# Attention block: the sink enters the row maximum as its start value, logits are kept negated, GpSimd makes the low weight parts in quarters, and the gate sigmoids and output splits stand elsewhere

## Chip, cores and metric

The kernel runs on one core of one Trainium2 chip. The metric is device time in microseconds for one launch. The program is one long sequence of engine instructions in a fixed order: TensorE (PE) multiplies, VectorE (DVE), ScalarE (ACT) and GpSimd (POOL) prepare and drain its operands, and SyncE (SP) issues the weight loads.

## What is computed

Two transformer blocks on 512 tokens of width 1024, all in float32. The first block (retention, spatial gating unit, convolutional MLP) is not touched. The second block is where the change lies:

```python
proj = einsum('bld,de->ble', h, w_in[l])
o_a = dsa_branch(a_q, a_k, a_v, i_q, i_k, i_w, topk)   # indexer picks 128 keys per query, causal
o_b = swa_branch(b_q, b_k, b_v, sinks[l])              # window of 128 keys, one sink logit per head
y_a = einsum('ble,ed->bld', o_a, w_branch_a[l])
y_b = einsum('ble,ed->bld', o_b, w_branch_b[l])
mix = sigmoid(g_a) * y_a + sigmoid(g_b) * y_b
x = x + einsum('bld,de->ble', mix, w_out[l])
h2 = rmsnorm(x, mlp_norm_w[l])
u = relu(einsum('bld,df->blf', h2, w_up[l]))
x = x + einsum('blf,fd->bld', u * u, w_down[l])
```

In `swa_branch` the sink is one more logit of every softmax row: it enters the row's maximum and the row's sum, and its own probability is dropped.

## The kernel before

**Split products.** Every large product is made of three TensorE passes over a high and a low part (`mm`, lines 245 to 247). A weight unit (512 KB, 128 partitions x 1024) is loaded into `wr`, ScalarE copies it to the high part `wh` (line 220), and another engine subtracts to get the low part `wl` (line 208, `Stream.flush`). That engine is `W.eng`: VectorE for most of the program, GpSimd from line 1172 to line 1260, that is from the second block's attention up to the end of the product with `w_out_2`. Three raw buffers and five split buffers let the stream run up to three units ahead of TensorE (`LEAD`). Activations are split in the same way by `split` (lines 147 and 148): ScalarE writes the high part, VectorE subtracts for the low part.

**Order.** Nothing is scheduled at run time: the order of instructions on each engine is the order in which the Python program emits them. Class `Weave` holds side tasks (generators) with countdowns; the dense loops call `tick` after a fixed number of matmuls, and a task whose countdown is over emits its next piece there. An attention head pair is such a task (`attend`, line 1052), started every `SWA_EVERY` = 0.75 or `ATT_EVERY` = 0.7 units of dense work; the task waits `LAG_N`, `LAG_T` and `LAG_V` units between its pieces. Each engine runs its own list strictly in order, so an instruction that waits holds all that is behind it on its engine.

**One attend.** For a query tile and two heads: TensorE makes the logits (line 1019); VectorE adds the mask, writes the logits to `pr` and takes the row maximum `mx` (line 1072, one instruction for each head); in the window branch it takes the maximum with the sink (line 1075); it negates the maximum to `nm` (line 1077); ScalarE makes exp(logit + nm) with row sums (line 1080); in the window branch VectorE makes sink + nm and ScalarE its exponential `es` (lines 1084, 1085), which VectorE adds to `sums` (line 1088); VectorE takes the reciprocal `rs` (line 1090); ScalarE scales the rows (line 1092); TensorE transposes (line 1101), ScalarE copies the result to `pT` (line 1103), TensorE multiplies with the values (line 1110), and `put` drains that product: in the window branch by `split` into `ob`, in the other branch by a copy into `oaT` (line 1215), which is split in four pieces after all attends are done (line 1227).

**Around the attends.** The dense work that covers them: the remaining projections, the gate logits `Y` (line 1211), the product with `w_branch_b_2` (line 1217) and the gate logits `Ya` (line 1223). `gate` copies each feature tile of logits out of PSUM (line 1205) and after every fourth applies the sigmoid to 128x2048 values at once (line 1207); exp and sigmoid need different tables on ScalarE, so a sigmoid between exponentials brings two table loads. After the attends come the product with `w_branch_a_2` (line 1243), whose `ev` multiplies by the gate (VectorE, line 1233), adds `Y` (GpSimd, line 1234) and splits the sum into `mh` and `ml`; then the product with `w_out_2` (`down`, line 1259), whose first unit needs the features in order and whose last tiles start the norms `norm_T` for `w_up_2` (lines 466 to 489).

## Time and profile before

| | us |
|---|---|
| median of 3 runs | 1611.67 (1609.97 to 1612.4) |
| profiled execution, time | 1611.67 |
| profiled execution, span from first to last instruction | 1609.9 |
| TensorE busy | 1579.2 (98%) |
| VectorE busy | 765.8 (48%) |
| ScalarE busy | 614.1 (38%) |
| GpSimd busy | 329.8 (20%) |

The profiled execution's time equals the median; 1.8 us of it lie around the span. TensorE's share of busy time is modelled from pipelined matmuls, so a stall shows best as idle time with the instruction that ended it, and as a granted clock below 1.00 in a stretch. The granted clock has two levels, 2.4 GHz (1.00) and 1.2 GHz (half); a mean of 0.96 over a stretch mixes the two.

### The profile page before, as it was taken

What the parts mean: (1) busy time and instruction counts of PE and PEld (TensorE: products, weight loads), DVE (VectorE), ACT (ScalarE), POOL (GpSimd) and SP (SyncE); (2) the same over time, 40 slices, a digit from 0 to 9 for tenths busy, and PEclk for the clock granted to TensorE, in tenths of its full rate; (3) what the DMA queues carried; (4) which work ended last, traced back from release to release, by engine and by line L of the source; (5) the groups of instructions that cost most, each with busy time, mean ns of one, the idle gap of its engine ahead of it and who ended that gap; (6) DMA issues with size and microseconds to landing.
All of it is one profiled execution on the core that took longest, in us unless ns stands there. A gap on an engine that the chain in (4) does not pass through costs nothing.

```text
span 1609.9 us, 19821 instructions
## 1 busy us (share of the span) xinstructions
PE 1579.2 (98%) x7868; PEld 1323.8 (82%) x7868; DVE 765.8 (48%) x1315; ACT 614.1 (38%) x1014; POOL 329.8 (20%) x292
## 2 busy tenths in 40 slices
PE   9999999999999999999999999999999999999998
PEld 8888888888888888888888887777877988888886
DVE  4247322453546544456336788768543322233333
ACT  4233223322324433344234366675833322333222
POOL 1015000341003221212004443333245210110000
PEclk9999999999999999999999999999999999999999
DMA  6322333212442233334321412222233333333221
GB/s 184 118 92 66 92 118 91 69 54 89 131 144 59 86 96 101 92 92 140 126 92 49 143 53 53 79 58 75 66 119 103 92 105 88 96 121 97 97 92 53
DMA packets 187249, 151.77 MB, mean 94 GB/s; under 512 B 5218, under 2 KB 157410, under 8 KB 186644
## 3 DMA queue, kind: packets, MB, share of 16 engines
q1 hardware_dynamic: 185648, 145.06, 29.8%
q0 software_dynamic: 1504, 5.44, 1.0%
q8 instruction: 62, 1.02, 0.3%
q14 instruction: 31, 0.25, 0.0%
q10 hardware_dynamic: 4, 0.00, 0.0%
HBM read 146.29 MB, written 4.19 MB: 93 GB/s over the span
## 4 chain that ended last, share of the span: by engine, by line
PE 82%; DVE 8%; ACT 4%; issue 2%; POOL 2%; ACTq 0%; POOLq 0%; DVEq 0%
PE ps L245 25%; PE ps L247 25%; PE ps L246 25%; PE ps L279 1%; ACT pr L1080 1%; DVE work L1036 1%; PE ps L1019 1%; PE ps L1110 1%; ACT wh L220 1%; PE ps L487 1%; POOL Ya L1234 1%; PE ps L772 1%; DVE sums L1088 1%; PE ps L1101 1%; POOL rstd L460 1%
## 5 line engine op out<-in xcount | busy, mean ns | idle before, releaser
L220 ACT ACTIVATE wh<-wr 128x1024 fp32r<-128x1024 f32 (+1 forms) x259 | 270.8, 1051 | 249.5 <-PE ps L247 131.1
L208 DVE TENSOR_TENSOR wl<-wr,wh 128x1024 fp32r<-128x1024 f32 (+1 forms) x212 | 258.0, 1227 | 174.5 <-ACT wh L220 174.4
L245 PE MATMUL ps<-wh,ls 128*128 128x512 f32 x432 | 168.2, 389 | 0.0
L247 PE MATMUL ps<-wh,ls 128*128 128x512 f32 x432 | 168.1, 389 | 0.0
L246 PE MATMUL ps<-wl,ls 128*128 128x512 f32 x432 | 168.1, 389 | 0.0
L208 POOL TENSOR_TENSOR wl<-wr,wh 128x1024 fp32r<-128x1024 f32 x47 | 114.5, 2445 | 134.5 <-ACT wh L220 127.7
L245 PE MATMUL ps<-h2Th,wh 128*128 128x512 f32 (+1 forms) x352 | 132.7, 377 | 0.0
L246 PE MATMUL ps<-h2Tl,wh 128*128 128x512 f32 (+1 forms) x352 | 132.7, 377 | 0.0
L247 PE MATMUL ps<-h2Th,wl 128*128 128x512 f32 (+1 forms) x352 | 132.7, 377 | 0.0
L245 PE MATMUL ps<-hTh,wh 128*128 128x512 f32 (+1 forms) x256 | 97.7, 382 | 0.0
L247 PE MATMUL ps<-hTh,wl 128*128 128x512 f32 (+1 forms) x256 | 96.4, 376 | 0.0
L246 PE MATMUL ps<-hTl,wh 128*128 128x512 f32 (+1 forms) x256 | 96.2, 376 | 0.0
L245 PE MATMUL ps<-h3Th,wh 128*128 128x512 f32 (+1 forms) x256 | 96.2, 376 | 0.0
L246 PE MATMUL ps<-h3Tl,wh 128*128 128x512 f32 (+1 forms) x256 | 96.2, 376 | 0.0
L247 PE MATMUL ps<-h3Th,wl 128*128 128x512 f32 (+1 forms) x256 | 96.2, 376 | 0.0
L247 PEld LDWEIGHTS ps<-wh,ls 128*128 128x128 f32 x432 | 81.1, 188 | 16.8
L246 PEld LDWEIGHTS ps<-wl,ls 128*128 128x128 f32 x432 | 81.1, 188 | 16.8
L245 PEld LDWEIGHTS ps<-wh,ls 128*128 128x128 f32 x432 | 81.1, 188 | 16.7
L903 ACT ACTIVATE hid<-ps,cols 128x512 f32<-128x512 f32 x44 | 34.3, 780 | 142.2 <-PE ps L247 142.2
L904 DVE SCALAR_TENSOR_TENSOR hid<-ps,cols,hid 128x511 f32<-128x511 f32 x44 | 33.0, 750 | 114.3 <-ACT hid L903 114.3
L911 POOL TENSOR_TENSOR act<-hid 128x512 f32<-128x512 f32 x22 | 46.1, 2094 | 192.3 <-DVE hid L906 176.7
L246 PEld LDWEIGHTS ps<-h2Tl,wh 128*128 128x128 f32 x352 | 66.3, 188 | 12.2
(316 smaller groups left out, 3297.9 us busy)
## 6 DMA issues: line engine op xcount, KB each, us to landing
wr<-in_w_in_dram SPq DMA_DIRECT2D x86, 512.0 KB, 3.8
wr<-in_w_up_dram SPq DMA_DIRECT2D x76, 512.0 KB, 4.0
wr<-in_w_down_dram SPq DMA_DIRECT2D x54, 512.0 KB, 3.6
wr<-in_w_out_dram SPq DMA_DIRECT2D x16, 512.0 KB, 3.7
wr<-in_w_sgu_o_dram SPq DMA_DIRECT2D x8, 512.0 KB, 4.2
wr<-in_w_ret_o_dram SPq DMA_DIRECT2D x8, 512.0 KB, 4.2
g<-in_rows_dram POOLq DMA_DIRECT2D x6, 512.0 KB, 7.3
x<-in_x_dram SPq DMA_DIRECT2D x4, 512.0 KB, 5.7
```

The lines of the kernel that those rows point to most:

```text
L208: eng.tensor_tensor(lo, self.raw.pop(i), hi.bitcast(F32), ALU.subtract)
L220: nc.scalar.activation(hi, self.raw[self.n_hi], AF.Copy)
L245: nc.tensor.matmul(q, lhs[0], rhs[0], start=start, stop=False)
L246: nc.tensor.matmul(q, lhs[0], rhs[1], start=False, stop=False)
L247: nc.tensor.matmul(q, lhs[1], rhs[0], start=False, stop=stop)
L279: nc.tensor.matmul(q[:, :256], wslice(u, k, 0, P)[i], act.at(k, 0, 256)[j], start=(i + j + k == 0), stop=(i == 1 and k == K - 1))
L460: nc.gpsimd.tensor_tensor(r, r, nhalf, ALU.pow)
L487: nc.tensor.transpose(q[:, i * P:(i + 1) * P], xn[:, k * P:(k + 1) * P], ident)
L772: nc.tensor.matmul(o, kz[:, d, c - d, :], vc[c], start=True, stop=True)
L903: nc.scalar.activation(o, q, AF.Identity, bias=col("conv_b", f), scale=col("conv_w1", f))
L904: nc.vector.scalar_tensor_tensor(o[:, 1:], q[:, :T - 1], col("conv_w0", f), o[:, 1:], ALU.mult, ALU.add)
L911: nc.gpsimd.tensor_tensor(act[fa // 4][:, fa % 4, :], a, b, ALU.mult)
```

## The change

- **Sink and sign.** The instruction that adds the mask now multiplies by -1 and takes the minimum, so `pr` holds negated logits and its row result is already `nm`. In the window branch its start value is the negated sink (`nsink`, made once, 128x8), so the sink is in the extremum from the start. Lines 1075 and 1077 go away. The exponential runs with scale -1. The sink's exponential is made by ScalarE from `sinkb` with bias `nm`, one 128x1 instruction for each head, so line 1084 goes away and line 1085 becomes two instructions.
- **Quarters.** While `W.eng` is GpSimd, each low weight part is made by four instructions on 128x256 instead of one on 128x1024.
- **`W.eng`** goes back to VectorE ahead of the product with `w_branch_a_2`, no longer behind the product with `w_out_2`.
- **Gate sigmoids of `Ya`** are no longer applied inside the dense loop: the first half's stands after all attends, the second half's behind feature 1 of the product with `w_branch_a_2`. Those of `Y` stay.
- **Output splits.** Each attend of the first branch writes its result at once as high and low part (`oa`), so `oaT` and the four splits behind the attends go away.
- **Last tile.** For the last query tile of that branch VectorE scales the rows, no longer ScalarE.
- **`ATT_EVERY`** goes from 0.7 to 0.65.

```diff
-ATT_EVERY = 0.7
+ATT_EVERY = 0.65
...
-                eng = nc.gpsimd if i in ON_POOL else self.eng
-                eng.tensor_tensor(lo, self.raw.pop(i), hi.bitcast(F32), ALU.subtract)
+                raw = self.raw.pop(i)
+                if self.eng is nc.gpsimd and i not in ON_POOL:
+
+                    w = hi.shape[1] * hi.shape[2] // 4
+                    l_, r_, h_ = (a.rearrange("p k n -> p (k n)") for a in (lo, raw, hi.bitcast(F32)))
+                    for p_ in range(4):
+                        s = slice(p_ * w, (p_ + 1) * w)
+                        nc.gpsimd.tensor_tensor(l_[:, s], r_[:, s], h_[:, s], ALU.subtract)
+                else:
+                    eng = nc.gpsimd if i in ON_POOL else self.eng
+                    eng.tensor_tensor(lo, raw, hi.bitcast(F32), ALU.subtract)
...
+    nsink = const.tile([P, 8], F32, name="nsink")
+    nc.vector.tensor_scalar(nsink, sinkb, -1.0, None, op0=ALU.mult)
...
-        mx = sm(2, "mx")
+        nm = sm(2, "nm")
         for i in range(2):
             q = ps()
             scores(q, qT, 2 * j + i, t, (kT[0][:, g], kT[1][:, g]), k0 * P, n)
             nc.vector.tensor_tensor_reduce(
-                pr[i][:, :n], q[:, :n], mask, 1.0, -3.0e38, ALU.add, ALU.max, mx[:, i:i + 1])
-        if br == 1:
-            nc.vector.tensor_tensor(mx, mx, sinkb[:, 2 * j:2 * j + 2], ALU.max)
-        nm = sm(2, "nm")
-        nc.vector.tensor_scalar(nm, mx, -1.0, None, op0=ALU.mult)
+                pr[i][:, :n], q[:, :n], mask, -1.0,
+                nsink[:, 2 * j + i:2 * j + i + 1] if br == 1 else 3.0e38, ALU.add, ALU.min, nm[:, i:i + 1])
         sums = sm(2, "sums")
         for i in range(2):
-            nc.scalar.activation(pr[i][:, :n], pr[i][:, :n], AF.Exp, bias=nm[:, i:i + 1],
+            nc.scalar.activation(pr[i][:, :n], pr[i][:, :n], AF.Exp, bias=nm[:, i:i + 1], scale=-1.0,
                                  accum_out=sums[:, i:i + 1])
         if br == 1:
             es = sm(2, "es")
-            nc.vector.tensor_tensor(es, sinkb[:, 2 * j:2 * j + 2], nm, ALU.add)
-            nc.scalar.activation(es, es, AF.Exp)
+            for i in range(2):
+                nc.scalar.activation(es[:, i:i + 1], sinkb[:, 2 * j + i:2 * j + i + 1], AF.Exp,
+                                     bias=nm[:, i:i + 1])
...
         for i in range(2):
-            nc.scalar.activation(pr[i][:, :n], pr[i][:, :n], AF.Copy, scale=rs[:, i:i + 1])
+            if br == 0 and t == NT - 1:
+                nc.vector.tensor_scalar(pr[i][:, :n], pr[i][:, :n], rs[:, i:i + 1], None, op0=ALU.mult)
+            else:
+                nc.scalar.activation(pr[i][:, :n], pr[i][:, :n], AF.Copy, scale=rs[:, i:i + 1])
...
-    def gate(dst):
+    def gate(dst, now=True):
...
-            if f % 4 == 3:
+            if now and f % 4 == 3:
                 nc.scalar.activation(dst[f // 4], dst[f // 4], AF.Sigmoid)
...
-    oaT = bigt([P, 4, T], "oaT")
+    oa = Branch()
     att = wv.spawn(stagger(
-        [attend(0, t, j, lambda j, a, b, q: nc.vector.tensor_copy(oaT[:, j, a:b], q))
+        [attend(0, t, j, lambda j, a, b, q: split(oa.hi[:, j, a:b], oa.lo[:, j, a:b], q))
...
-    dense_a(a_units(w_in_2, 2120, 8), hT2, gate(Ya))
+    dense_a(a_units(w_in_2, 2120, 8), hT2, gate(Ya, False))
     wv.finish([att, idx_task])
-    oa = Branch()
-    for j in range(4):
-        split(oa.hi[:, j, :], oa.lo[:, j, :], oaT[:, j, :])
+    nc.scalar.activation(Ya[0], Ya[0], AF.Sigmoid)
+    W.eng = nc.vector
...
         split(h_[:, f % 4, :], l_[:, f % 4, :], ya(f))
+        if f == 1:
+            nc.scalar.activation(Ya[1], Ya[1], AF.Sigmoid)
...
     down(w_out_2, KD, mix_pair, fin)
-    W.eng = nc.vector
```

The order moves in three places. The line numbers in the second fence of each are those of the changed kernel.

ScalarE at the end of the attends, from the last row scalings or weight copies to the first high part of the mix (`mh`), before and now:

```order
L1092 ACTIVATE pr<-pr,rs 128x512 x2
L1103 ACTIVATE pT<-ps 128x512 x2
L1205 ACTIVATE Ya<-ps 128x512
L1207 ACT_TABLE_LOAD
L1207 ACTIVATE Ya<-Ya 128x2048
L1103 ACTIVATE pT<-ps 128x512 x2
L147 ACTIVATE obh<-oaT 128x512 x4
L147 ACTIVATE mh<-Ya 128x512
```

```order
L147 ACTIVATE obh<-ps 128x128
L1116 ACTIVATE pT<-ps 128x512 x2
L1218 ACTIVATE Ya<-ps 128x512
L1116 ACTIVATE pT<-ps 128x512 x2
L147 ACTIVATE obh<-ps 128x128 x2
L1238 ACT_TABLE_LOAD
L1238 ACTIVATE Ya<-Ya 128x2048
L147 ACTIVATE mh<-Ya 128x512
L229 ACTIVATE wh<-wr 128x1024
L147 ACTIVATE mh<-Ya 128x512
L1250 ACTIVATE Ya<-Ya 128x2048
```

The table load and the sigmoid stood ahead of the last two copies to `pT`; now they stand behind the last attend's output copies, and the second sigmoid behind the second `mh`.

The low weight parts inside the product with `w_branch_a_2`: GpSimd before, VectorE now (GpSimd keeps only the eight additions there):

```order
L208 TENSOR_TENSOR wl<-wr,wh 128x1024 x20
L386 DMA g<-in_rows_dram 128x1024 x2
L1234 TENSOR_TENSOR Ya<-Ya,Y 128x512 x2
L208 TENSOR_TENSOR wl<-wr,wh 128x1024
L1234 TENSOR_TENSOR Ya<-Ya,Y 128x512 x2
```

```order
L148 TENSOR_TENSOR obl<-ps,obh 128x128 x3
L1245 TENSOR_TENSOR Ya<-Ya,ps 128x512
L148 TENSOR_TENSOR ml<-Ya,mh 128x512
L1245 TENSOR_TENSOR Ya<-Ya,ps 128x512
L148 TENSOR_TENSOR ml<-Ya,mh 128x512
L217 TENSOR_TENSOR wl<-wr,wh 128x1024
L1245 TENSOR_TENSOR Ya<-Ya,ps 128x512
```

Each `wl` leaves GpSimd's row of additions and stands on VectorE behind every second `ml`, ahead of the next feature's multiplication with the gate.

VectorE in the norms of the last two token tiles ahead of `w_up_2`, before and now:

```order
L1255 TENSOR_TENSOR xs<-xs,ps 128x512
L478 SCALAR_TENSOR_TENSOR xn<-xs,rstd,g 128x1024
L1255 TENSOR_TENSOR xs<-xs,ps 128x512
L148 TENSOR_TENSOR h3Tl<-ps,h3Th 128x4x128 x2
L1255 TENSOR_TENSOR xs<-xs,ps 128x512
L478 SCALAR_TENSOR_TENSOR xn<-xs,rstd,g 128x1024
L208 TENSOR_TENSOR wl<-wr,wh 128x1024
L148 TENSOR_TENSOR h3Tl<-ps,h3Th 128x4x128 x2
```

```order
L1269 TENSOR_TENSOR xs<-xs,ps 128x512
L487 SCALAR_TENSOR_TENSOR xn<-xs,rstd,g 128x1024
L1269 TENSOR_TENSOR xs<-xs,ps 128x512
L217 TENSOR_TENSOR wl<-wr,wh 128x1024 x2
L148 TENSOR_TENSOR h3Tl<-ps,h3Th 128x4x128 x2
L1269 TENSOR_TENSOR xs<-xs,ps 128x512
L487 SCALAR_TENSOR_TENSOR xn<-xs,rstd,g 128x1024
L217 TENSOR_TENSOR wl<-wr,wh 128x1024
L148 TENSOR_TENSOR h3Tl<-ps,h3Th 128x4x128 x2
```

Two low weight parts, which GpSimd made before, now stand ahead of the third tile's `h3Tl` and so ahead of the fourth tile's `xn`.

## Rows read from the trace of the kernel before

**Rows 1.** The page, part 1: busy us (share of the span) xinstructions of each engine.
```profile
PE 1579.2 (98%) x7868; PEld 1323.8 (82%) x7868; DVE 765.8 (48%) x1315; ACT 614.1 (38%) x1014; POOL 329.8 (20%) x292
```

**Rows 2.** Stretch, length; busy us (x) of PE, PEld, DVE, ACT, POOL; granted clock; DMA.
```profile
960.00:1080.00 120.00, 111.22 (x671) 90.10 (x670) 90.37 (x296) 76.04 (x195) 41.54 (x22) 1.00 0.22 62
...
1080.00:1160.00 80.00, 80.00 (x452) 64.38 (x452) 55.71 (x157) 53.88 (x123) 26.10 (x11) 1.00 0.24 67
...
1160.00:1240.00 80.00, 75.04 (x373) 60.31 (x372) 26.78 (x39) 32.94 (x49) 38.80 (x24) 0.96 0.36 119
```

**Rows 3.** Who waited for whom, PE: us in total, times, longest us.
```profile
PE ps L1101 <- ACT pr L1092: 3.8, 3, 3.1
```

**Rows 4.** Timeline, 987 to 1012 us: start us, us, engine, what [idle before <-releaser].
```profile
987.55 0.17 DVE L1077 TENSOR_SCALAR nm<-mx 128x2 f32<-128x2 f32 x1
...
1001.92 0.74 POOL L510 TENSOR_TENSOR rk<-rope 128x256 f32<-128x256 f32 x1 [5.10 <-DVE rope L504]
...
1004.56 4.70 POOL L208 TENSOR_TENSOR wl<-wr,wh 128x1024 fp32r<-128x1024 f32 x2
...
1005.73 1.24 DVE L1075 TENSOR_TENSOR mx<-mx,sinkb 128x2 f32<-128x2 f32 x1
1007.00 2.29 DVE L1077 TENSOR_SCALAR nm<-mx 128x2 f32<-128x2 f32 x1
...
1009.38 0.51 ACT L1080 ACTIVATE pr<-pr,nm 128x256 f32<-128x256 f32 x1 [4.28 <-DVE nm L1077]
...
1011.46 0.41 PE L493 MATMUL ps<-ident,rk 128*128 128x128 f32 x2 [2.86 <-ACT pT L1103]
```

**Rows 5.** Groups by line, VectorE and ScalarE, 930 to 1215 us: busy us, mean ns.
```profile
L1077 DVE TENSOR_SCALAR nm<-mx 128x2 f32<-128x2 f32 x32 | 19.1, 596 | 1.1
...
L1088 DVE TENSOR_TENSOR sums<-sums,es 128x2 f32<-128x2 f32 x16 | 11.3, 704 | 0.0
...
L1049 DVE TENSOR_SCALAR work<-work 128x512 f32<-128x512 f32 x1 | 0.4, 419 | 0.0
...
L1085 ACT ACTIVATE es<-es 128x2 f32<-128x2 f32 x16 | 3.0, 188 | 0.0
```

**Rows 6.** Timeline, end of the attention, 1171 to 1177 us: ScalarE, then TensorE.
```profile
1171.06 1.28 ACT L1207 ACT_TABLE_LOAD   x1
1172.35 1.91 ACT L1207 ACTIVATE Ya<-Ya 128x2048 f32<-128x2048 f32 x1
1174.16 1.07 ACT L1103 ACTIVATE pT<-ps 128x512 f32<-128x512 f32 x2
...
1174.80 1.15 PE L1110 MATMUL ps<-pT,va 128*64 128x128 f32 x16 [2.35 <-ACT pT L1103]
...
1176.93 0.61 PE L246 MATMUL ps<-obl,wh 128*128 128x512 f32 x1 [0.56 <-DVE obl L148]
```

**Rows 7.** Timeline, product with w_branch_a_2 and after, 1181 to 1214 us.
```profile
1181.35 0.69 DVE L1233 TENSOR_TENSOR Ya<-Ya,ps 128x512 f32<-128x512 f32 x1 [2.66 <-PE ps L247]
...
1184.72 0.68 DVE L1233 TENSOR_TENSOR Ya<-Ya,ps 128x512 f32<-128x512 f32 x1
1187.46 2.21 DVE L148 TENSOR_TENSOR ml<-Ya,mh 128x512 fp32r<-128x512 f32 x1 [2.06 <-ACT mh L147]
1189.59 0.68 DVE L1233 TENSOR_TENSOR Ya<-Ya,ps 128x512 f32<-128x512 f32 x1
...
1211.42 9.85 POOL L208 TENSOR_TENSOR wl<-wr,wh 128x1024 fp32r<-128x1024 f32 x4
...
1213.84 0.50 PE L246 MATMUL ps<-wl,mh 128*128 128x512 f32 x1 [1.80 <-POOL wl L208]
```

**Rows 8.** Timeline, last norms ahead of w_up_2, 1251 to 1258 us.
```profile
1251.96 1.29 DVE L148 TENSOR_TENSOR h3Tl<-ps,h3Th 128x512 fp32r<-128x512 f32 x2 [0.85 <-ACT h3Th L147]
...
1257.29 1.22 DVE L208 TENSOR_TENSOR wl<-wr,wh 128x1024 fp32r<-128x1024 f32 x1
...
1257.52 1.06 PE L487 MATMUL ps<-ident,xn 128*128 128x128 f32 x8
```

## The prediction

> **What bounds the kernel now.** I read the page first: TensorE is busy for 1579.2 us, 98% of the span, and no other engine passes half [rows 1]. So the change can only win what TensorE loses by waiting, or by running at the lower clock level. The table by stretch then shows where that is in the second block [rows 2]: from 960 to 1080 us (window attention) TensorE is busy for 111.22 of 120 us, so 8.8 us are idle; from 1080 to 1160 us (the other attention branch, under dense work) it is never idle; from 1160 to 1240 us it is idle for 5.0 us and the granted clock is 0.96. A mean of 0.96 over 80 us is 0.04 x 80 = 3.2 us of lost array time, at the 1.2 GHz level. Together 17 us lie open in places the change touches.
>
> Third, the timeline says why. Around 1005 us VectorE's `mx`, two numbers per partition, takes 1.24 us, and `nm`, just as small, takes 2.29 us, though it took 0.17 us at 987.55 us [rows 4]. Over the stage `nm` has a mean of 596 ns and `sums` one of 704 ns [rows 5]. In the same microseconds GpSimd makes two low weight parts, 4.70 us in all [rows 4]: `mx` ends as the first of them ends (1004.56 + 2.35 = 1006.9 us), `nm` as the second ends (1009.26 us). So some VectorE instructions stand still until GpSimd's current instruction is over. ScalarE's exponential then starts at 1009.38 us after 4.28 us of idle time, and TensorE waits 2.86 us for a PSUM buffer that ScalarE has not drained [rows 4]. The largest other wait of this kind is for ScalarE's row scaling, 3.8 us in three waits, the longest 3.1 us, at the first window attend [rows 3].
>
> **The sum, part by part.** The profiled execution took 1611.67 us, which is also the median of the runs; the sum starts there.
>
> *Window attention.* Sixteen `mx`, 32 `nm` and 16 sink additions leave VectorE, and what still stands still does so behind a quarter. A quarter costs 0.74 us by the 128x256 addition [rows 4], so the longest single wait falls from 2.4 to about 0.7 us. At 1011.46 us the chain was `mx`, then `nm`, then the exponential: both are gone, so I count all 2.9 us. Of the 3.1 us at the first attend I count 1.1: three small instructions at about 0.2 us, and half a microsecond less of standing still for the indexer's accumulation ahead of them. Of the other 2.8 us (8.8 less these two) I count a third, 0.9 us, since the sigmoids of `Y`, with their table loads, stay in the ScalarE queue there. That makes 4.9 us. I give back 0.9: TensorE arrives sooner at the next late operand, and ScalarE gains sixteen instructions of 188 ns for the second sink exponential, 3.0 us over the stage [rows 5]. **-4.0 us.** Bounds: -7.9 (all but 0.9 of the idle time), and +2 if the quarters bring more waits than the three instructions removed.
>
> *End of the attends.* Before, ScalarE loads the sigmoid table (1.28) and makes the sigmoid (1.91) ahead of the last two copies to `pT`; TensorE waits 2.35 us for them, then 0.56 us for the first split of `oaT` [rows 6], and runs at the lower level afterwards, half of the 3.2 us above: 1.6 us. That is 4.5 us. Now these copies stand ahead of the table load, and three quarters of the output are split before the last attend ends. What stays is the way from the last transposes through two copies (1.07 us for both [rows 6]), about half covered by the product of the attend before: 0.5 us. **-4.0 us.** Bounds: -4.5 and -1 (the clock falls all the same, and 2 us of waits stay).
>
> *Product with `w_branch_a_2`.* The chain is serial: VectorE multiplies, GpSimd adds, ScalarE rounds, VectorE subtracts. A feature takes 3.37 us (1181.35 to 1184.72), a pair 8.24 us (to 1189.59), because one `ml` stands still for GpSimd's weight part and takes 2.21 us, where a VectorE instruction of that shape takes 0.69 [rows 7]. The weight part of the third unit of `w_out_2` is the first of the four that start at 1211.42 us; it ends near 1213.9 us, 32.5 us after the chain began, and TensorE waits 1.80 us for it [rows 7] and pays the other 1.6 us at the lower level. Now VectorE makes the weight part (1.22 us [rows 8]) inside the same chain: a pair is 2 x 3.37 + 1.22 = 7.96 us, and that third unit is ready after 3 x 7.96 + 2 x 3.37 + 1.22 = 31.8 us, only 0.7 us sooner. Against that the chain starts later: 1.28 + 1.91 us of table load and sigmoid now stand behind the last output copy, 3.7 us with the 0.5 us of copies before them, where the first feature's product is there after about 2.8 us (an estimate: 12 passes of 512 columns at 2.4 GHz, and 0.2 us on the way); that is 0.9 us later. **+0.2 us**: the stall of 1.8 us and its lower clock stay. Bounds: -3.4 (both go) and +1.6.
>
> The Trainium skill, "ScalarE: Activation LUTs", section "What ACT_TABLE_LOAD costs", adds to the 1283 ns of the load a drain of about 1380 ns at every switch; by it the sigmoid would end 1.4 us later, and the sum would be 1.4 us worse. The trace disagrees: the sigmoid starts 0.01 us after the load ends [rows 6].
>
> *Norms ahead of `w_up_2`.* Two weight parts of 1.22 us move onto VectorE between the third tile's `xn` and its `h3Tl`. `h3Tl` had 0.85 us of idle time ahead of it, so 2.4 - 0.9 = 1.5 us of delay go down to the fourth tile's `xn`, which ended just ahead of the weight part at 1257.29 us and which TensorE's transposes took up at 1257.52 us, with no slack [rows 8]. **+1.4 us.** Bounds: 0 and +2.4.
>
> *The rest at nothing.* The second branch's attends now use ScalarE and VectorE for each output split; from 1080 to 1160 us these are busy for 53.88 and 55.71 of 80 us [rows 2], and two table loads and a sigmoid leave ScalarE there. The last tile's row scaling on VectorE costs 419 ns a piece by the 128x512 `L1049` [rows 5], in a stretch where that engine has run out of key searches. If this cover were gone, each such step would be paid as in the window stage. `nsink` is one instruction of about 0.2 us. `ATT_EVERY` shifts early attends only; the last four wait for the key search.
>
> Sum: -4.0 - 4.0 + 0.2 + 1.4 = -6.4, so **1605.3 us**, 0.4% faster. Its own range is 1602.5 to 1608. A measurement of this kernel can tell about 0.2%, 3.2 us, from no change.
>
> **The rivals.**
>
> *A, the stalls go more fully.* Window stage -7.2, end of the attends -4.5, and the 1.8 us stall with its clock loss (-3.4) goes because the chain starts on time; norms +1.4. Sum -13.7: 1598.0 us. For it: the idle times are there [rows 2]. Against: the chain's arithmetic gives only 0.7 us.
>
> *B, quarters do not let VectorE in between.* Then what is left (`sums`, splits, accumulations) stands still for 4 x 0.74 = 3.0 us instead of 2.4, and the window stage gains only 1.0 us from the instructions removed. Sum -1.0 - 4.0 + 0.2 + 1.4 = -3.4: 1608.3 us. Against it: `mx` ran at the boundary between two back-to-back GpSimd instructions [rows 4]. The Trainium skill, "GPSIMD Engine Reference", section "2.1 Instruction dispatch", says that a GpSimd core begins the next instruction as soon as its own share is done, without waiting for the other cores, so that boundary need not be free; by that rule rival B would be the case, and the trace agrees only in that GpSimd lost almost nothing there (2 x 2.35 us).
>
> *C, the change does not do what it says.* TensorE meets the next late operand everywhere, and the sigmoid behind the attends stalls the mix as much as it stalled the attends: window -1, end -1, mix +0.2, norms +1.4. Sum -0.4: 1611.3 us.
>
> *D, slower: GpSimd falls behind.* Its 32 weight parts of the stage cost 2.96 instead of about 2.4 us each, more if every quarter first lets a VectorE instruction finish. If a unit's low part then lands 0.5 us too late for TensorE, 32 x 0.5 = 16 us are added to 1605.3: 1621; at 0.3 us, 1614.9 us, which I take. It decides once a part takes longer than TensorE spends on a unit, about 245 / 32 = 7.7 us. Against: GpSimd is busy for 41.54 of 120 us there [rows 2], and units are prepared three ahead.
>
> **How the numbers follow.** Chances: forecast 0.54, A 0.15, B 0.13, C 0.09, D 0.09. Range 1598.0 to 1610.5: from A's time up to between B and C; it leaves out C, D and the lower half of A's spread, with parts of their weight inside. Faster by over 0.2%: the forecast, A, and somewhat over half of B, 0.77. Within 0.2%: C and the rest of B, 0.14. Slower: D, 0.09.
>
> **What would show it.** Right: 128x256 weight parts near 0.74 us on GpSimd; `sums` well below 704 ns; idle time of TensorE from the first attend to 1080 us at 4 to 5 us; no wait above 1 us for `pT` at the last attend, and no low clock there; a wait of about 2 us for `wl` in the product with `w_out_2`; about 1.4 us in front of the fourth tile's transposes. Wrong: waits for `wl` from GpSimd inside the attention (D); VectorE instructions of 2 us beside quarters (B); idle time of TensorE between 1080 and 1160 us.

## The result, and the profile after

The changed kernel takes 1594.7 us (median of 4 runs, 1592.59 to 1595.24) against 1612.01 us before (4 runs, 1609.97 to 1612.4): a ratio of 0.9899 with an interval of 0.9887 to 0.9912. It is 17.3 us faster where 6.4 were forecast, and below the forecast range of 1598.0 to 1610.5. The profiled execution took 1595.02 us, with a span of 1593.3 us.

First the page of the changed kernel, part 1, which answers to [rows 1]:

```profile
PE 1573.6 (99%) x7868; PEld 1321.3 (83%) x7868; DVE 740.3 (46%) x1268; ACT 613.6 (39%) x1032; POOL 317.3 (20%) x376
```

TensorE's busy time fell by only 5.6 us, the span by 16.6: the rest was idle time. VectorE's fell by 25.5 us, although it now makes 224 low weight parts and not 212, each of some 1.2 us. It has 47 instructions fewer, and many that are left must have become shorter.

Second the stretches of the changed kernel, with the columns of [rows 2]. The work now comes some 10 us earlier, so 960 to 1070 answers to 960 to 1080 before.

```profile
960.00:1070.00 110.00, 108.98 (x668) 89.53 (x667) 69.37 (x247) 81.17 (x210) 49.26 (x64) 1.00 0.25 68
1070.00:1150.00 80.00, 80.00 (x455) 64.27 (x454) 47.73 (x150) 51.16 (x133) 29.46 (x42) 1.00 0.24 67
1150.00:1170.00 20.00, 20.00 (x144) 16.30 (x142) 5.29 (x14) 11.78 (x21) 7.21 (x10) 1.00 0.58 211
1195.00:1200.00 5.00, 3.00 (x14) 2.12 (x13) 3.42 (x4) 2.52 (x3) 0.88 (x1) 1.00 0.12 6
```

In the window attention 8.8 us of idle time have become 1.0. Up to 1170 us TensorE never stops again. At 1195 us it stops for 2.00 us, and the clock stays at 1.00; at 1240 us it stops for 1.32 us (the line is shown with the norms, below).

Third, who waited for whom, the waits of TensorE in the changed kernel, which answer to [rows 3]:

```profile
PE ps L496 <- DVE xn L487: 5.8, 7, 1.4
...
PE ps L255 <- DVE wl L217: 3.5, 2, 2.0
...
PE ps L1114 <- ACT pr L1105: 1.0, 1, 1.0
```

The 3.8 us for `pr` are 1.0, one wait at the first window attend. The 2.00 us at 1195 are a wait for `wl`, now VectorE's.

The time can be placed by the start of the same matmuls in both timelines, because TensorE's work between them is the same. "Scores" is the first window score product, "PV" the last window product with the values, "branch a" the first matmul with `w_branch_a_2`, "w_out" its first matmul with `mh`. The norms' stage runs from the last of these to the last matmul of `w_up_2`. The first two landmarks, the kernel before and then the changed kernel:

```profile
957.81 0.56 PE L1019 MATMUL ps<-bkT,bqT 128*128 128x128 f32 x4
...
1070.05 0.66 PE L1110 MATMUL ps<-pT,work 128*64 128x128 f32 x8
```

```profile
957.12 0.56 PE L1030 MATMUL ps<-bkT,bqT 128*128 128x128 f32 x4
...
1059.97 0.66 PE L1123 MATMUL ps<-pT,work 128*64 128x128 f32 x8
```

| us between | before | after | change | forecast |
|---|---|---|---|---|
| scores to PV | 112.24 | 102.85 | -9.4 | -4.0 |
| PV to branch a | 105.82 | 103.23 | -2.6 | |
| branch a to w_out | 24.35 | 21.91 | -2.4 | -4.0, with the row above |
| w_out, first to last `mh` | 49.80 | 47.89 | -1.9 | +0.2 |
| last `mh` to last `h3T` | 177.80 | 179.07 | +1.3 | +1.4 |

That makes -15.0 of the span's -16.6. Another 0.8 come between the second block's first transposes of `xn` (878.73 us before, 878.84 after) and the scores. There the kernel before has this wait of TensorE. Two small VectorE instructions (`ik`, 128x64) had taken 2.03 and 2.32 us beside two weight parts of GpSimd, 0.38 and 0.65 us in the changed kernel, and `hl` came behind them:

```profile
920.43 0.63 PE L493 MATMUL ps<-ident,hl 128*128 128x128 f32 x4 [0.79 <-DVE hl L148]
```

The wait is there (0.67 to 0.82 us) in every kernel below in which GpSimd makes the parts whole or in halves, and in none with quarters. The remaining 0.8 lie in what follows `w_up_2` and in code that the change does not touch, and are less than runs of one kernel differ by (2.4 us before).

### The profile page after: what moved, and what is told of

The parts are those of the page before. It is cut to its first block, busy times and chain, and to the rows that moved or that the text cites. A ratio compares the mean times of both kernels' runs of the same rounds, so it can differ in the third digit from the quotient of the medians.

```text
span 1593.3 us, 19894 instructions
## 1 busy us (share of the span) xinstructions
PE 1573.6 (99%) x7868; PEld 1321.3 (83%) x7868; DVE 740.3 (46%) x1268; ACT 613.6 (39%) x1032; POOL 317.3 (20%) x376
## 4 chain that ended last, share of the span: by engine, by line
PE 90%; DVE 4%; ACT 2%; POOL 2%; issue 2%; ACTq 0%; POOLq 0%; DVEq 0%
PE ps L254 27%; PE ps L256 27%; PE ps L255 27%; PE ps L1030 1%; PE ps L1123 1%; PE ps L1114 1%; PE ps L502 1%; PE ps L288 1%; POOL Ya L1246 1%; PE ps L781 1%; ACT junk L475 1%; POOL rstd L469 1%; DVE wl L217 1%; PE ps L496 1%; DVE y L533 1%
## 5 line engine op out<-in xcount | busy, mean ns | idle before, releaser
L217 DVE TENSOR_TENSOR wl<-wr,wh 128x1024 fp32r<-128x1024 f32 (+1 forms) x224 | 272.4, 1227 | 177.0 <-ACT wh L229 176.9
L214 POOL TENSOR_TENSOR wl<-wr,wh 128x256 fp32r<-128x256 f32 x128 | 94.9, 774 | 112.0 <-ACT wh L229 102.9
L256 PEld LDWEIGHTS ps<-h2Th,wl 128*128 128x128 f32 x352 | 66.2, 188 | 12.3
```

What stands on the lines that cost most here:

```text
L214: nc.gpsimd.tensor_tensor(l_[:, s], r_[:, s], h_[:, s], ALU.subtract)
L217: eng.tensor_tensor(lo, raw, hi.bitcast(F32), ALU.subtract)
L256: nc.tensor.matmul(q, lhs[1], rhs[0], start=False, stop=stop)
```

## The experiments

Each run stands against the kernel before on the same chip: 1610.83 us for the four that have one or more parts of the change alone, 1609.79 for the halves, the end moves without `W.eng`, `W.eng` alone and the spacing, 1609.47 for the rest. Theory 1 is the prediction's: a VectorE instruction of some kinds stands still until GpSimd's current instruction is over. Theory 2 is that the attends gained because their chain has fewer instructions.

### The parts of the change alone

**Quarters alone**, on the kernel before:

```diff
-                eng.tensor_tensor(lo, self.raw.pop(i), hi.bitcast(F32), ALU.subtract)
...
+                    for p_ in range(4):
+                        s = slice(p_ * w, (p_ + 1) * w)
+                        nc.gpsimd.tensor_tensor(l_[:, s], r_[:, s], h_[:, s], ALU.subtract)
```

> The kernel before with GpSimd's low weight parts in quarters and nothing else. Theory 1 (some VectorE instructions stand still until GpSimd's current instruction is over, and that is what TensorE waited for in the window attention): the longest standing time falls from 2.4 to 0.75 us, nm's mean from 596 to under 300 ns, and about 6 us of the window stage's 10 us go: 1606 us. Theory 2 (the gain comes from three fewer instructions in each attend's chain, and the standing is hidden by queues): 1612 us, within 1.5 us of before, or slower by the 0.5 us more that each part costs GpSimd.

Measured: 1600.88 us, 9.95 below before, ratio 0.994 (0.9928 to 0.9953). The groups of this kernel, 930 to 1180 us, with the columns of [rows 5]:

```profile
L1086 DVE TENSOR_SCALAR nm<-mx 128x2 f32<-128x2 f32 x32 | 8.1, 252 | 1.1
...
L1097 DVE TENSOR_TENSOR sums<-sums,es 128x2 f32<-128x2 f32 x16 | 5.2, 327 | 0.0
...
L214 POOL TENSOR_TENSOR wl<-wr,wh 128x256 fp32r<-128x256 f32 x115 | 84.6, 768 | 114.3 <-ACT wh L229 105.5 <-PE ps L1119 8.7
```

Not one instruction left VectorE, and yet scores to PV takes 105.56 us, 6.7 less, although the clock was at 0.67 from 965 to 970 us, behind a wait at the first attend. (What the stage would take at the full clock is not shown: the kernel with `W.eng` alone, below, lost twice that clock there and took no longer for it.) `nm` fell from 596 to 252 ns and `sums` from 704 to 327 [rows 5]. Theory 2 cannot give this; Theory 1's 6 us for the stage are near, and what the time won beyond them lies elsewhere (see the halves). The price is GpSimd's: a quarter takes 768 ns, so four take 3.07 us where one piece took 2.43 (the 29 pieces there before were busy for 70.2 us, the 115 quarters for 84.6), and no wait for a `wl` of GpSimd came up in the attention.

**Sink and sign alone**, on the kernel before:

```diff
-            nc.vector.tensor_tensor(mx, mx, sinkb[:, 2 * j:2 * j + 2], ALU.max)
...
-        nc.vector.tensor_scalar(nm, mx, -1.0, None, op0=ALU.mult)
...
+                pr[i][:, :n], q[:, :n], mask, -1.0,
+                nsink[:, 2 * j + i:2 * j + i + 1] if br == 1 else 3.0e38, ALU.add, ALU.min, nm[:, i:i + 1])
```

> The kernel before with the sink as start value and negated logits, and nothing else. Theory 1: the 16.7 us that nm and mx stood still leave VectorE, so about 6 us are gained here too, and the two parts overlap: 1606 us. Theory 2: this part alone makes the whole window gain, 10 us: 1602 us. If neither holds (the instructions were not on the path): 1611 us.

Measured: 1603.15 us, 7.7 below before, ratio 0.9956 (0.9943 to 0.9968). Scores to PV takes 105.13 us, 7.1 less, although `sums` still takes 712 ns. The time lies between Theory 1's 1606 and Theory 2's 1602 and decides nothing by itself; with the quarters' run, where no instruction went, the account is that the two parts remove the same loss in two ways: one shortens the stand of `mx` and `nm`, the other takes these two out of the chain. So each brings about 7 us alone in that stage, and the whole change 9.4.

**The whole change without quarters:**

```diff
-                if self.eng is nc.gpsimd and i not in ON_POOL:
...
-                else:
-                    eng = nc.gpsimd if i in ON_POOL else self.eng
-                    eng.tensor_tensor(lo, raw, hi.bitcast(F32), ALU.subtract)
+                eng = nc.gpsimd if i in ON_POOL else self.eng
+                eng.tensor_tensor(lo, self.raw.pop(i), hi.bitcast(F32), ALU.subtract)
```

> The changed kernel with whole low weight parts on GpSimd, 128x1024 each. Theory 1: sums and the splits with two SBUF inputs stand still for up to 2.4 us again, sums' mean returns to about 700 ns, and 3 to 4 us are lost: 1598 us. Theory 2: 1595 us, as the changed kernel.

Measured: 1597.56 us, ratio 0.9917 (0.9903 to 0.993), 13.3 below before. On top of the rest, the quarters are worth 2.3 us from scores to PV (105.15 against 102.85), and nothing in the four stages behind it, which agree within 0.02 us.

**The end moves alone** (sigmoids, output splits, last tile's scaling, `W.eng`, `ATT_EVERY`), on the kernel before:

```diff
-ATT_EVERY = 0.7
+ATT_EVERY = 0.65
...
-    dense_a(a_units(w_in_2, 2120, 8), hT2, gate(Ya))
+    dense_a(a_units(w_in_2, 2120, 8), hT2, gate(Ya, False))
...
+    nc.scalar.activation(Ya[0], Ya[0], AF.Sigmoid)
+    W.eng = nc.vector
```

> The kernel before with the last part of the change alone: gate sigmoids of Ya and output splits moved, W.eng back to VectorE earlier, rows of the last tile scaled on VectorE, ATT_EVERY 0.65; whole weight parts and the old sink and sign. Both theories: the window stage stays as it was, and the end gains what the landmarks of the two traces show behind the window stage, 17.3 - 10.1 = 7 us: 1605 us. Should the low clock at the end of the attends come back, 1607 us.

Measured: 1607.47 us, ratio 0.9982 (0.9973 to 0.9991), 3.4 below before. That is the time of the second expectation but not its cause, for the clock stays up at the end of the attends. From branch a on it is the changed kernel (21.90, 47.86 and 179.07 us). From PV to branch a it takes 105.95 us, no less than before: there TensorE waits 0.94 us for a `pT` at 1137.6 us, where whole weight parts meet the closer spacing of the attends. With the old spacing and the same whole parts (end moves without `W.eng` and `ATT_EVERY`, below) this stretch takes 103.73 us. In the run above, which has the closer spacing and adds sink and sign, that wait is gone.

### How long is a stand, and who stands

**Halves**, on the kernel before: the edit of the quarters with 2 in place of 4, shown here against the kernel with quarters alone.

```diff
-                    w = hi.shape[1] * hi.shape[2] // 4
+                    w = hi.shape[1] * hi.shape[2] // 2
...
-                    for p_ in range(4):
+                    for p_ in range(2):
```

> The kernel before with GpSimd's low weight parts in two halves, nothing else. Theory 1 (a VectorE instruction stands still until GpSimd's current instruction ends): the mean of nm falls in proportion between 596 ns (one piece) and 252 ns (four), to 350 to 420 ns, and sums from 704 to 430 to 520 ns. For the time there are two readings of it: 1a, the loss of TensorE grows with the length of the longest stand: half of the 10 us that the quarters won, 5 us below before. 1b, the attends have some slack, and a stand costs only beyond it: then halves win nearly all, 8 to 10 us below before.

Measured: 1599.94 us, ratio 0.9935 (0.9923 to 0.9946), 9.85 below before. The groups of this kernel, 930 to 1180 us:

```profile
L1086 DVE TENSOR_SCALAR nm<-mx 128x2 f32<-128x2 f32 x32 | 12.3, 384 | 1.1
...
L1097 DVE TENSOR_TENSOR sums<-sums,es 128x2 f32<-128x2 f32 x16 | 7.1, 446 | 0.0
...
L214 POOL TENSOR_TENSOR wl<-wr,wh 128x512 fp32r<-128x512 f32 x58 | 76.2, 1336 | 122.1 <-ACT wh L229 122.1
```

With pieces of 2.43, 1.34 and 0.77 us `nm` takes 596, 384 and 252 ns, and `sums` 704, 446 and 327: the stand follows the length of GpSimd's piece. The time does not: halves win 6.1 us from scores to PV and quarters 6.7 (106.16 and 105.56 us, with a like stretch at the lower clock in both). TensorE's wait of 2.86 us at 1011 us [rows 4] is gone with halves as with quarters, and the one at the first attend, 3.06 us before, is 2.11 us with quarters and, in the kernel with halves,

```profile
966.36 0.62 PE L1110 MATMUL ps<-ident,pr 128*128 128x128 f32 x2 [2.40 <-ACT pr L1101]
```

That fits reading 1b: an attend has slack, and only a stand beyond it costs. The totals of the two runs say less, because they hold more than this stage: in these profiles 2.3 us of the quarters' gain and 3.6 of the halves' lie ahead of the second block, in code that neither edit touches, and another 2.6 and 3.7 between first and last `mh`.

**Everything on VectorE**, on the changed kernel:

```diff
-    W.eng = nc.gpsimd
```

> The changed kernel, but all low weight parts are made by VectorE in one instruction each, in the attention too. Theory 1 (the window stage lost its time to VectorE standing still behind GpSimd): sums near 0.17 us, no long stands; but 14 parts of 1.22 us enter VectorE's queue from 960 to 1070 us (69 + 17 = 86 of 110 us busy), each a delay of up to 1.2 us for what is behind it, less than the 2.4 us of GpSimd's whole part and more than its quarter: 1595 to 1598. Theory 2 (the gain came from the shorter chain of small instructions, and VectorE's load is what counts): VectorE is the busiest engine there again, and the window stage gives back most of its 10 us: 1601 to 1606.

Measured: 1597.07 us, ratio 0.9922 (0.9908 to 0.9937), 12.4 below before. First the stretches, then the groups from 930 to 1180 us of this kernel:

```profile
960.00:1070.00 110.00, 109.78 (x671) 90.09 (x670) 80.67 (x259) 80.53 (x209) 8.90 (x8) 1.00 0.25 68
1070.00:1150.00 80.00, 77.82 (x437) 61.44 (x436) 57.00 (x152) 48.73 (x128) 0.00 (x0) 1.00 0.25 67
```

```profile
L217 DVE TENSOR_TENSOR wl<-wr,wh 128x1024 fp32r<-128x1024 f32 x30 | 36.5, 1217 | 0.7 <-ACT wh L229 0.5
...
L1098 DVE TENSOR_TENSOR sums<-sums,es 128x2 f32<-128x2 f32 x16 | 3.4, 215 | 0.0
```

From 960 to 1070 us VectorE is busier than in the changed kernel (80.67 against 69.37 us), and scores to PV is the shortest of all, 102.16 us, with no wait of TensorE: neither GpSimd's help nor a low load was needed there, only that nothing stands for long. The loss came behind it: PV to branch a takes 106.54 us, 3.3 more than in the changed kernel. In that stage TensorE waits three times for `pT`, 1.7 us in all, while VectorE's busy time has gone up from 47.73 to 57.00 of 80 us.

### The end of the attends, and the lower clock

**The end moves without `W.eng` and `ATT_EVERY`**, on the kernel before:

```diff
-    dense_a(a_units(w_in_2, 2120, 8), hT2, gate(Ya))
+    dense_a(a_units(w_in_2, 2120, 8), hT2, gate(Ya, False))
...
+    nc.scalar.activation(Ya[0], Ya[0], AF.Sigmoid)
```

> The kernel before with the gate sigmoids moved, the output split in each attend and the row scaling of the last tile on VectorE; weight parts whole and with GpSimd up to the end of the product with w_out_2. Theory 1 (these moves remove the stall at the end of the attends and its low clock, and nothing else): from the first matmul with w_branch_a_2 to the first with w_out_2 it takes 21.9 us as in the changed kernel, against 24.35 before; the wait at the third unit of w_out_2 stays near 1.8 us with a stretch at the low clock level behind it, no norm wait is added: 3 to 4 us below before. Rival (the low clock of the second wait is an after-effect of the first): the wait stays, the clock stays up, 5 us below before.

Measured: 1604.73 us, ratio 0.9963 (0.9951 to 0.9975), 5.1 below before. Branch a to w_out takes 21.90 us, as in the changed kernel, PV to branch a 103.73. So these moves alone remove the stall at the end of the attends with its lower clock; which of the three moves does how much was not run. The second low stretch is still there. TensorE's two main waits in the product with `w_out_2` (a third, 0.21 us for a `wl`, comes 4.5 us ahead of them), then the stretches, of this kernel:

```profile
1204.86 0.50 PE L245 MATMUL ps<-wh,mh 128*128 128x512 f32 x1 [0.35 <-DVE Ya L1235]
...
1208.55 0.50 PE L246 MATMUL ps<-wl,mh 128*128 128x512 f32 x1 [1.81 <-POOL wl L208]
```

```profile
1205.00:1210.00 5.00, 3.19 (x12) 2.30 (x13) 2.17 (x1) 2.53 (x3) 5.00 (x3) 0.93 0.07 6
1210.00:1215.00 5.00, 5.00 (x17) 3.98 (x17) 0.00 (x0) 1.09 (x2) 5.00 (x3) 0.73 0.58 208
```

A clock of 0.93 and then 0.73 means that part of these 10 us ran at the 1.2 GHz level: 0.07 x 5 + 0.27 x 5 = 1.7 us lost. So it is no after-effect of the first stall, and the rival falls, although its time fits (5.1 below). The five stages of its profile account for 3.2 of the 5.1, as the theory had it.

**`W.eng` alone**, on the kernel before:

```diff
     wv.finish([att, idx_task])
+    W.eng = nc.vector
...
     down(w_out_2, KD, mix_pair, fin)
-    W.eng = nc.vector
```

> The kernel before with only the weight parts given back to VectorE ahead of the product with w_branch_a_2. Theory 1: ml no longer stands still there, the stall and the low clock at the end of the attends stay (24.3 us from the first matmul with w_branch_a_2 to the first with w_out_2), the wait at the third unit of w_out_2 stays near 2 us, norms +1.3: between 0 and 1 us above before; if the clock stays up behind that wait, 1 us below.

Measured: 1609.26 us, ratio 0.9988 (0.998 to 0.9996), 0.5 below before. The stall at the end of the attends stays (2.35 us, and 25.22 us from branch a to w_out). From first to last `mh` it takes 47.11 us, 2.7 less than before: TensorE waits 1.28 us for VectorE's `wl`, and the clock stays at 1.00. The last stage costs 1.3 us more (179.08). So with this one edit the second low stretch is not there in the profile, and the norms' wait is.

The same profile has a warning. Up to the end of the attends this kernel's instructions are those of the kernel before, and its wait at the first attend is as long (3.07 us against 3.06). There the clock stayed at 1.00 from 960 to 1080 us [rows 2]; here it fell behind that wait, and again at 1010 us:

```profile
970.00:975.00 5.00, 5.00 (x19) 4.01 (x18) 4.90 (x12) 2.95 (x10) 2.95 (x2) 0.68 0.23 55
...
1010.00:1015.00 5.00, 4.77 (x16) 3.81 (x17) 2.80 (x17) 2.15 (x10) 1.46 (x2) 0.66 0.27 79
```

That is 0.32 x 5 + 0.34 x 5 = 3.3 us of clock, yet scores to PV takes 112.36 us against 112.24. The later waits took it up: 1.96 us instead of 2.86 at 1010 us, and three more, of 0.4 to 0.6 us, are gone. So a low stretch among waits can cost next to nothing, and whether it comes can differ between two executions of the same instructions.

**GpSimd longer**, on the changed kernel:

```diff
-    W.eng = nc.vector
     state = {}
...
     down(w_out_2, KD, mix_pair, fin)
+    W.eng = nc.vector
```

> The changed kernel, but the low weight parts stay with GpSimd (in quarters) up to the end of the product with w_out_2. Theory 1 (each remaining wait there is set by the chain of the late operand; the parts on VectorE only moved work): the third unit of w_out_2 is waited for 1 to 1.5 us instead of 2.0, as in the kernel that had only the quarters (1.14 us at 1200 to 1205), the wait of 1.3 us for the fourth norm goes, no low clock: about 2 us faster than the changed kernel (1594.7), 1592.5. Theory 2 (the early return to VectorE is what keeps TensorE at the high clock level there): the low level comes back after that wait, +1.6 us, and with ml behind the quarters the chain is no faster: 1595 to 1597.

Measured: 1593.5 us, ratio 0.9896 (0.988 to 0.9913), 16.0 below before: the same as the change. TensorE's waits for `wl` in the product with `w_out_2`, this kernel:

```profile
1197.14 0.50 PE L255 MATMUL ps<-wl,mh 128*128 128x512 f32 x1 [0.82 <-POOL wl L214]
...
1198.97 0.51 PE L255 MATMUL ps<-wl,mh 128*128 128x512 f32 x1 [0.86 <-POOL wl L214]
```

Two waits of 0.8 us take the place of one of 2.0, at a clock of 1.00. Both theories were half right: the low level did not come back, but not 2 us were won either; the last stage gave back 0.44 us (178.63), not 1.3.

**Spacing of the attends**, on the changed kernel:

```diff
-ATT_EVERY = 0.65
+ATT_EVERY = 0.7
```

> The changed kernel with the attends of the first branch spaced as before (0.7 units, not 0.65). Theory 1: that spacing moves only attends that have room, so the end of the attends stays where it is and the time is that of the changed kernel within 1 us, about 16 to 17 us below before. Rival: the closer spacing is what lets the last attends come on time: the stall ahead of the last values product comes back in part, 1 to 3 us.

Measured: 1595.59 us, ratio 0.9909 (0.9896 to 0.9921), 14.2 below before. Its profile has PV to branch a at 103.78 us, 0.55 more, and a last wait of 0.25 us for `pT`: less than a timing of this kernel can tell.

### The two waits that were left

**The weight part inside the chain**, on the changed kernel:

```diff
         nc.gpsimd.tensor_tensor(ya(f), ya(f), y(f), ALU.add)
+        W.flush()
         h_, l_ = state[f // 4]
```

> The changed kernel, but in the product with w_branch_a_2 VectorE makes a low weight part while it would wait for the addition of GpSimd (2.06 us of idle time), not behind ml. Theory 1 (the 2.0 us wait at the third unit of w_out_2 is the serial chain of 7.9 us for two features): the pair falls to about 6.8 us, the third unit is there some 3 to 4 us sooner and the wait goes: 1592.7, 2.0 below the changed kernel. Rival (the wait is set by when the weight lands or by ScalarE's copy of it): the wait stays and the time is 1594.7.

Measured: 1590.11 us, the fastest of all, ratio 0.9879 (0.9864 to 0.9894), 19.4 below before. Its interval still touches the change's, but the trace shows the gain in its place: first to last `mh` takes 45.51 us, 2.4 less, with no wait for `wl`; the other four stages agree within 0.01 us. The reason is the order, not the speed that was expected of the chain: the fourth `wl` starts at 1193.16 us, ahead of the last `ml` (1196.22), where the changed kernel makes it behind that `ml` (1197.19), and a pair of features takes 7.64 us (1166.25 to 1173.89), not 6.8. The timeline of VectorE and GpSimd in this kernel says why:

```profile
1167.03 1.29 POOL L1246 TENSOR_TENSOR Ya<-Ya,Y 128x512 f32<-128x512 f32 x1 [9.47 <-DVE Ya L1245]
...
1170.22 1.22 DVE L217 TENSOR_TENSOR wl<-wr,wh 128x1024 fp32r<-128x1024 f32 x1
...
1170.38 2.20 POOL L1246 TENSOR_TENSOR Ya<-Ya,Y 128x512 f32<-128x512 f32 x1 [2.07 <-DVE Ya L1245]
```

GpSimd's addition takes 1.29 us alone, and 2.20 beside VectorE's weight part: it stands until that ends at 1171.44 us. The stand goes both ways.

**And the last norms' weight parts on GpSimd**, on top of that:

```diff
             norms.append(run(norm_T(t, xrow(t), g_mlp, h3T)))
+            if t == 1:
+                W.eng = nc.gpsimd
...
     down(w_out_2, KD, mix_pair, fin)
+    W.eng = nc.vector
```

> As the one before, and the two low weight parts ahead of the last norms go back to GpSimd in quarters. Theory 1 (the 1.3 us that TensorE waits for the fourth xn is these two parts, 2 x 1.22 us on VectorE less its slack): both waits go, 3.3 us below the changed kernel: 1591.4. Rival (the xn is late by the norm's own chain; or its instructions stand still behind GpSimd's quarters): 1592.7 or more.

Measured: 1591.14 us, ratio 0.9884 (0.9869 to 0.9899), 18.3 below before, no different from the kernel without this step. The timeline ahead of the fourth tile's transposes, this kernel:

```profile
1229.20 6.67 POOL L214 TENSOR_TENSOR wl<-wr,wh 128x256 fp32r<-128x256 f32 x8
...
1234.78 0.18 ACT L475 ACTIVATION_READ_ACCUMULATOR junk<-xs 128x1 f32 x1
...
1235.96 0.19 POOL L468 TENSOR_SCALAR rstd<-ss 128x1 f32<-128x1 f32 x1
...
1236.81 1.28 DVE L487 SCALAR_TENSOR_TENSOR xn<-xs,rstd,g 128x1024 f32<-128x1024 f32 x1 [3.09 <-POOL rstd L469]
...
1238.24 0.95 PE L496 MATMUL ps<-ident,xn 128*128 128x128 f32 x7 [0.89 <-DVE xn L487]
```

The wait is 0.89 us instead of 1.33. GpSimd makes the norm's `rstd` as well. ScalarE had its input ready at 1234.96 us, but GpSimd was held by the eight quarters, 6.67 us, until 1235.87. In the kernel before two whole parts took 5.83 us there and the wait was nil [rows 8]; with four halves, 6.10 us, it was 0.31. So here the price of cutting shows, and the rival was nearer: the `xn` is late because a step of its norm comes behind GpSimd's quarters, in GpSimd's own order.

## Why the prediction was wrong

**Window attention: the mechanism right, the size wrong.** Of the 10.9 us between forecast and result this stage has 5.4, the end of the attends 1.0 and the product with `w_out_2` 2.1. The failed step is the sum under *Window attention*: -4.0, bounds -7.9 to +2; measured -9.4. The mechanism, VectorE standing still behind GpSimd's current instruction, holds with no run against it. The Trainium skill, "SBUF — State Buffer", section "Who interferes with whom", gives it a name: a VectorE instruction with two SBUF inputs, or in a two-port mode, and a GpSimd instruction that reads SBUF share ports, and whichever starts first holds them to its end. The traces agree, with `nm` at 2.29 us [rows 4] and the addition at 2.20 us above. In the changed kernel, around 1000 us:

```profile
999.77 4.91 POOL L214 TENSOR_TENSOR wl<-wr,wh 128x256 fp32r<-128x256 f32 x7
...
1000.39 0.51 ACT L1089 ACTIVATE pr<-pr,nm 128x256 f32<-128x256 f32 x1 [0.28 <-DVE nm L1084]
...
1000.68 0.08 DVE L1084 DVE_READ_ACCUMULATOR2_ANT nm<- 128x1 f32 x1
...
1002.72 0.59 DVE L1098 TENSOR_TENSOR sums<-sums,es 128x2 f32<-128x2 f32 x1
```

Seven quarters run in a row, the negated extremum is there 0.08 us after its instruction, and the exponential waits 0.28 us for it, not 4.28. `sums` still stands, 0.59 us here. `rs` (128x2, one input) took 161 or 162 ns on the mean in every kernel, whatever GpSimd did. Over 930 to 1180 us, the groups of the changed kernel:

```profile
L1098 DVE TENSOR_TENSOR sums<-sums,es 128x2 f32<-128x2 f32 x16 | 6.4, 399 | 0.0
...
L214 POOL TENSOR_TENSOR wl<-wr,wh 128x256 fp32r<-128x256 f32 x115 | 85.5, 776 | 111.1 <-ACT wh L229 102.0 <-PE ps L256 9.0
```

The wait of 2.9 us was counted in full, rightly; three other steps of the sum were too small. Of the 3.1 us at the first attend 2.1 went, not 1.1. Of the other 2.8 us of idle time all went, not "a third". And nothing was given back, where 0.9 was taken off, mainly on the ground that TensorE meets the next late operand: TensorE has no wait at all from the first attend to 1170 us, as is to be expected if a stand costs only beyond an attend's slack. That is 3.8 us. The bound was wrong as well. It was idle time alone, and -7.8 of the -9.4 is idle time; the last 1.6 lay in time that the profile counts as busy (103.52 us from scores to PV before, 101.88 after, for the same matmuls).

**End of the attends: right in kind, 1.0 too small.** Forecast -4.0, measured -5.0. ScalarE's timeline there, changed kernel:

```profile
1161.03 1.09 ACT L1116 ACTIVATE pT<-ps 128x512 f32<-128x512 f32 x2
...
1163.31 0.28 ACT L147 ACTIVATE obh<-ps 128x128 fp32r<-128x128 f32 x1 [0.59 <-PE ps L1123]
...
1163.61 1.28 ACT L1238 ACT_TABLE_LOAD   x1
...
1164.90 1.92 ACT L1238 ACTIVATE Ya<-Ya 128x2048 f32<-128x2048 f32 x1
```

The copies to `pT` now run ahead of the table load, as the order shows, and TensorE no longer waits for them. The stall of 2.35 us, the 0.56 us for the split and 1.7 us of lower clock went; the 0.5 us counted for the two copies was not to be seen, since the stretch from 1150 to 1170 us has no idle time. These make 4.6 of the 5.0; the other 0.4 are not placed. The sigmoid again starts 0.01 us after the table load ends, so the drain that the prediction cited from the Trainium skill shows at this sigmoid in neither kernel's trace.

**Product with `w_branch_a_2`: the wait right, its clock wrong.** The failed step is "the stall of 1.8 us and its lower clock stay". The stall stayed:

```profile
1198.46 0.50 PE L255 MATMUL ps<-wl,mh 128*128 128x512 f32 x1 [2.00 <-DVE wl L217]
```

It is TensorE's wait in the timeline of the changed kernel. The chain was as computed: a pair takes 7.86 us against 7.96. But the lower level went, and with it 1.7 us; that is most of the -1.9 in place of +0.2. The other executions speak for the same: the mean granted clock was 0.998 in three executions of the changed kernel and 0.997 in the fourth, and 0.991 to 0.996 in the 39 of the kernel before that the experiments stand against. The waits and then the stretches of the kernel with sink and sign alone show the other case:

```profile
1202.63 0.50 PE L245 MATMUL ps<-wh,mh 128*128 128x512 f32 x1 [0.25 <-DVE Ya L1233]
...
1206.32 0.50 PE L246 MATMUL ps<-wl,mh 128*128 128x512 f32 x1 [1.80 <-POOL wl L208]
```

```profile
1200.00:1205.00 5.00, 4.27 (x18) 2.89 (x16) 1.65 (x3) 2.60 (x4) 2.93 (x3) 1.00 0.23 86
1205.00:1210.00 5.00, 3.68 (x11) 2.93 (x12) 1.81 (x1) 1.55 (x3) 5.00 (x3) 0.73 0.33 105
```

There, as in the kernel before, a wait of 0.25 us for VectorE's `Ya` comes 3.7 us ahead of the long one; two steps earlier in that chain an `ml` stood for 2.21 us behind GpSimd's weight part. The kernel with GpSimd longer had two waits too, 0.82 and 0.86 us, and kept the clock, and so did the one with quarters alone (0.28 and 0.86); a single wait of 2.00 us also kept it. What takes the clock down after the one and not after the other stays open: the runs show only that it did so in the three profiles with a short wait and one of 1.8 us (before, sink and sign alone, end moves without `W.eng`), and in no other at that place. In the window attention the same instructions with the same wait ended both ways, as the kernel with `W.eng` alone shows.

**Norms ahead of `w_up_2`: right.** Forecast +1.4, measured +1.3. The timeline of the changed kernel:

```profile
1234.01 2.36 DVE L217 TENSOR_TENSOR wl<-wr,wh 128x1024 fp32r<-128x1024 f32 x2
...
1236.28 1.29 DVE L148 TENSOR_TENSOR h3Tl<-ps,h3Th 128x512 fp32r<-128x512 f32 x2
...
1240.35 1.28 DVE L487 SCALAR_TENSOR_TENSOR xn<-xs,rstd,g 128x1024 f32<-128x1024 f32 x1 [2.19 <-POOL rstd L469]
...
1241.78 1.06 PE L496 MATMUL ps<-ident,xn 128*128 128x128 f32 x8 [1.32 <-DVE xn L487]
```

Two weight parts of 2.36 us in all push `h3Tl` and the fourth `xn` back, and TensorE waits 1.32 us. Giving them back to GpSimd in quarters won back only 0.44 us, as the last experiment shows.

**What was put at nothing** stayed so from 1070 to 1170 us (no idle time of TensorE) and for `ATT_EVERY` (within 0.55 us). The 0.8 us for `hl` ahead of the scores were not in the sum: it began at 960 us, but GpSimd makes the weight parts from some 45 us earlier on. **The rivals:** A had the right direction in every term (window -7.2, end -4.5, mix -3.4) and at 0.15 too small a chance, but its reason for the mix failed: the stall stayed and only the clock loss went. Even its time, 1598.0, is 3.3 too high. B falls: `nm` has a mean of 252 ns beside quarters, so VectorE does get in between them, and the Trainium skill's dispatch rule, on which B leaned, does not keep it out. C falls with the window and the end of the attends. D falls: no wait for GpSimd's `wl` in the attention, although a part took 28% longer (4 x 776 ns for 2.43 us).

## What to carry to other kernels

When small instructions of one engine stand behind long ones of another, measure how their mean time falls as the long one is cut: two pieces already won 6.1 of the 6.7 us that four won in the window attention, at a lower price for what stands behind them on the cut engine, and moving the long ones away won as much as four in that stage. (Halves were not run in the changed kernel.) Where one cause makes many waits, do not discount each for a next late operand, but ask for the slack of a chain: here all waits but the first went together. And where two parts of a change remove the same stand, their single gains add up to more than the whole (from scores to PV 6.7 and 7.1 us alone, 9.4 together). A clock seen in one profile is weak evidence: look at several executions before a low stretch is put down to an edit.

## What the runs showed of the hardware

- The stand behind the other engine goes both ways: VectorE's two-element `nm` took up to 2.29 us behind GpSimd, and GpSimd's addition 2.20 instead of 1.29 us behind VectorE's weight part.
- Cutting a GpSimd subtraction on 128x1024 costs: 2.43 us in one piece, 2 x 1.34 in halves, 4 x 0.77 in quarters.
- The lower clock level does not follow from the length of one wait: it came after 0.25 and 1.80 us, and not after a single 2.00 us at the same place of the program; and the same instructions with a wait of 3.06 and 3.07 us were followed by a clock of 1.00 in one profile and of 0.68 in another.
- Lower clock among waits cost next to nothing: with 3.3 us of it the window attention took 112.36 us, without it 112.24.
